# A two-layer trunk on one core: wider loads for the weights' squares, the input scale summed by TensorE, and the place of some memsets

## The chip, the core and the metric

The kernel runs on one core of one Trainium2 chip. The metric is device time in microseconds (us) of one execution. The kernel before took 1095.55 us (median of three runs, 1092.40 to 1097.43). One more execution was taken with the hardware profiler on: 1094.62 us, of which 1092.8 us are the span from the first to the last instruction that the profile shows. Differences of about 0.5% and more can be told from no change.

The engines are named as in the profile: PE is TensorE (PEld its weight loads), DVE is VectorE, ACT is ScalarE, POOL is GpSimd, and SP is the engine that issues most transfers. Each engine works through its own list of instructions in order.

## The reference

A sequence of 1024 tokens, 1024 wide, goes through two layers, each of which adds its result to the residual stream x, and then through a last RMS norm.

```python
def lru_mixer(h, ...):                       # layer 0
    u = h @ w_in                             # 1024 -> 2 * 1536
    xb, gate = u[..., :1536], u[..., 1536:]
    xc = causal_depthwise_conv(xb, conv_w, conv_b)          # 4 taps
    r = sigmoid(block_diag_linear(xc, wa, ba))              # 12 blocks of 128
    i = sigmoid(block_diag_linear(xc, wx, bx))
    log_a = -8.0 * r * softplus(-a_param)
    a = exp(log_a); bterm = sqrt(-expm1(2 * log_a)) * (i * xc)
    hs = scan over time of  s = a * s + bterm
    return (hs * silu(gate)) @ w_out

def fox_mixer(h, ...):                       # layer 1: 16 heads of 64
    u = h @ w_in                             # q, k, v, gate, and 16 forget logits
    cum = cumsum(log_sigmoid(f_logit + b_f))
    logits = q @ k.T / 8 + cum_q - cum_k, causal
    return (softmax(logits) @ v * silu(gate)) @ w_out

for i in range(2):
    h = rms_norm(x, norm_g[i])
    x = x + (lru_mixer if i == 0 else fox_mixer)(h, ...)
return rms_norm(x, final_g)
```

The arithmetic is float32. The kernel splits operands into a high and a low part and multiplies three of the four products (high by high, low by high, high by low).

## The kernel before

Activations lie transposed, channels on the 128 partitions and tokens along the free axis, in two halves of 512 tokens.

**First stage, layer 0 (0 to about 450 us).** A loop over twelve blocks `n` of 128 channels. For each block PE makes `ups` (the block's part of xb, `product`) and `gps` (its gate part), each 48 matmuls of 512 columns, and the two `gate` products. ACT and DVE make the convolution (`xc`), the sigmoids (`th`, `ti`), the recurrence and, a block later, the output y = state times gate, which is split into `yh` and `yl`. After each second block, `project_out` adds that pair's part of y @ w_out to x: the PE matmuls `ops`, which need `yh` and `yl`.

Weights come by a load on SP's queue into a tile `wf` (line 58 or 381), a cast on ACT to the high part `wh` (line 91), and a subtraction on POOL or DVE to the low part `wl` (line 102). The tiles `wf` have three buffers. While layer 0 runs, the list `spare` gives every fourth load one more buffer, with the tag `wx`, in another pool (lines 106 to 110).

Layer 1 works in float16 and needs bounds for its scales: sums of squares of its weights. They are made beside layer 0: `squares_of_weights` (line 407) loads a piece of 256 columns into `wvf` and squares it in place on ACT with `accum_out`, which also leaves the sum of each row. There are 129 such pieces, 32 of `wv`, 96 of `w1` and one of `wf`. They share a tag of two buffers, `wgf`, with the gate weights of `conv`. From block 2 on, the loop takes 4, 5 and 4 of them per block (lines 443, 457 and 466). The load and the square of a piece are written next to each other, so the square is the next user of what was just loaded.

**Between the layers (about 450 to 540 us).** For each half `h` of the tokens the last `ops` are added to x, ACT squares x (`sq`, with the row sums in eight columns of `xsq[h]`), and `input_scale(h)` makes the half's scale: `xsq` times g squared, a reduction of the eight columns to one on DVE (line 531), a sum over partitions by a matmul with ones (`xnorm`), a root (`unit_x`), a reciprocal and `gx`. `split_input(h)` then makes the float16 parts of the half, `hT[h]`, eight casts on ACT and eight on DVE (tiles `h`, line 542). PE goes on with the first of layer 1's projections (`gps`, `vps`). `values(0)` makes `vps`, the values with the forget logits: four tiles of the first half of the tokens, then four of the second, each 24 matmuls. DVE and ACT take them out of PSUM as `v`, and DVE takes the logits as `fz` (line 678). `fixed_rows` writes constants into the attention's operands: T by POOL, U by DVE (lines 603 to 606).

**Second stage, layer 1 (from about 540 us).** Attention head by head, with projections as fill, then the output.

What sets the order. The program is written as Python generators, and a scheduler puts each instruction on its engine's list by priority and by simulated times of its own. `tc.issue_after(x)` places what is written under it after instruction x; `tc.high_priority(offset=...)` raises priority. A buffer is given to its next user when its last reader is done, and the load for the next user waits on SP's queue for that, with everything behind it.

Of the kernel before, what the change touches and what calls it, by code (L numbers as in the profile page):

```python
# [19 lines left out]
P = 128  # L20
# [20 lines left out]
def trunk(ctx: ExitStack, tc: tile.TileContext, xt, w0, wg, wo0, pc, gn, gf, w1, wv, wf, bf, wo1, out):  # L41
# [11 lines left out]
    pe = [None]  # L53
# [137 lines left out]
    with ExitStack() as l0:  # L191
# [7 lines left out]
        spare.append(tmp)  # L199
# [101 lines left out]
        def conv(n, ups):  # L301
# [10 lines left out]
            wt = tmp.tile([P, 2, P], F32, tag="wgf", name="wgf", bufs=2)  # L312
# [94 lines left out]
        def squares_of_weights():  # L407

            todo = [(wv[g, :, k], vsq[:, g, k : k + 1]) for g in range(4) for k in range(KT)]
            todo += [(w1[b, :, 2 * j : 2 * j + 2], wsq[:, 4 * b + j : 4 * b + j + 1]) for b in range(24) for j in range(4)]  # L410
            todo.append((wf, root[:, 1:]))
            for src, to in todo:
                wt = tmp.tile([P, 256], F32, tag="wgf", name="wvf", bufs=2)
                if len(src.shape) == 3:
                    wt = wt[:, : src.shape[1] * src.shape[2]].rearrange("p (a b) -> p a b", b=src.shape[2])
                nc.sync.dma_start(wt, src)
                nc.scalar.activation(wt, wt, AF.Square, accum_out=to)  # L417
                yield

        wsquares = squares_of_weights()  # L420
        ys, fill, held = [], iter(()), {}
        for n in range(NB):
# [19 lines left out]
            if n > 1:  # L442
                take(wsquares, 4)
# [4 lines left out]
            conv(n, both)  # L448
            if n == 0:
# [4 lines left out]
            take(fill, 4)  # L454
            if n > 1:
                with tc.issue_after(state[n - 1]["last"].ins):
                    take(wsquares, 5)
                wn = list(weights(w0[NB + n - 1]))
                gps = held[n - 1] = two_banks("gps")
                for h in range(2):  # L460
                    product(gps[:, h], h, wn)
            if n:
                drain(silu(state[n - 1], held.pop(n - 1)))

                if n > 1:
                    take(wsquares, 4)
                with tc.issue_after(state[n]["tap"].ins):
                    recur(n - 1)
            take(fill, 4)
        gates(NB - 1)  # L470
# [8 lines left out]
        spare.clear()  # L479
# [27 lines left out]
        def weight_bounds():  # L507

            all_ = ps.tile([P, 161], F32, tag="O", name="wnorm")
            matmul(all_[:, 64:160], onesf, wsq, start=True, stop=True)  # L510
# [5 lines left out]
            for cs, to, n in ((slice(0, 64), bounds[:, :8], KT), (slice(64, 160), bounds[:, 8:], 4)):  # L516
# [11 lines left out]
        def input_scale(h):  # L528

            nc.vector.tensor_tensor(xsq[h], xsq[h], g2, ALU.mult)  # L530
# [3 lines left out]
            nc.scalar.activation(unit_x[h], all_, AF.Sqrt, bias=tiny, scale=1.0 / TOP / TOP)  # L534
            nc.vector.reciprocal(xsq[h][:, :1], unit_x[h])
            nc.vector.tensor_scalar(gx[h], gnt[:, 1], xsq[h][:, :1], None, ALU.mult)
# [11 lines left out]
        for h, cs in enumerate(halves):  # L548
# [41 lines left out]
    with ExitStack() as l1:  # L590
# [209 lines left out]
        fixed_rows()  # L800

# [6 lines left out]
        take(first, 8)  # L808
        drain(forget(0))
# [456 lines left out]
```

## Time and profile before

| | |
|---|---|
| runs | 1092.40, 1095.55, 1097.43 us; median 1095.55 |
| profiled execution | 1094.62 us; span 1092.8 us |
| busy in the span | PE 95%, PEld 66%, DVE 72%, ACT 61%, POOL 9% |
| squares of the weights on ACT (line 417) | 129, together 53.3 us, 413 ns each |
| ACT idle just before them, waiting for their loads | 85.6 us |
| first stage: PE busy, 100 to 200 us | 89.21 us |
| first stage: PE busy, 200 to 450 us | 245.95 us |
| between the layers: PE busy, 500 to 510 us | 5.38 us, at a granted clock of 0.66 |

How to read it. PE is busy nearly all the time, so the time can fall where PE waits, where its granted clock is below 1, or where it has less to do. A wait is put down to the instruction that ended last before it. In rows of a timeline the columns are start, duration, engine, line, operation, output and inputs, and count; a bracket gives the idle time before the row and its releaser. A float32 matmul leaves two records in the trace, so eight `sscol` instructions show as x16.

### The profile page before, as it was taken

The numbers are of one execution on the slowest core, as the hardware profiler recorded it, in microseconds if no ns is written. First come the engines' busy times: TensorE is split into PE (matmuls) and PEld (weight loads), VectorE is DVE, ScalarE is ACT, GpSimd is POOL, SyncE is SP. The second block draws the span as 40 slices with busy tenths as digits, with TensorE's granted clock in tenths as the row PEclk, the third lists the DMA queues.
The fourth block names the chain that finished last, engine by engine and source line by source line (L and its number), as shares of the span: only waits on it lengthen the run. The fifth ranks groups of instructions, "written<-read, shape, count | busy, mean of one in ns | idle before, by whom it ended". The sixth has DMA issues, their size and how long they took to land. (4 is left out here: it accounts for less than half of the span.)

```text
span 1092.8 us, 15397 instructions
## 1 busy us (share of the span) xinstructions
PE 1035.4 (95%) x5102; PEld 723.1 (66%) x5102; DVE 791.6 (72%) x1465; ACT 667.9 (61%) x1295; POOL 100.3 (9%) x87
## 2 busy tenths in 40 slices
PE   8998999999999999997899999999999899999997
PEld 6786777788777788765445557544665447577676
DVE  7788465666766768896778884888768884886675
ACT  8579556656565666465666664666556664754454
POOL 1311110222121211001000000000000000011100
PEclk9998999999999999998999999999999999999999
DMA  7212333233223331352578894689948886679994
GB/s 247 78 43 73 107 101 113 75 102 106 86 79 96 89 97 39 116 161 69 148 158 171 171 197 114 140 176 178 194 109 173 181 178 139 132 171 229 253 202 158
DMA packets 229023, 148.94 MB, mean 136 GB/s; under 512 B 162960, under 2 KB 192272, under 8 KB 228944
## 3 DMA queue, kind: packets, MB, share of 16 engines
q1 hardware_dynamic: 226544, 140.10, 52.8%
q0 software_dynamic: 2400, 7.87, 2.4%
q8 instruction: 40, 0.66, 0.3%
q14 instruction: 39, 0.32, 0.1%
HBM read 73.33 MB, written 11.67 MB: 78 GB/s over the span
## 5 line engine op out<-in xcount | busy, mean ns | idle before, releaser
L61 PE MATMUL gps<-h,w 128*128 128x512 f16 x1152 | 270.8, 382 | 2.2 <-DVE qkl L708 2.2
L61 PEld LDWEIGHTS <-w 128*128 128x128 f16 x1152 | 104.5, 98 | 128.6 <-issue 16.8
L861 ACT ACTIVATE p<-S,m 128x128 f32<-128x128 f32 (+7 forms) x128 | 94.2, 736 | 62.7 <-DVE m L856 38.9
L61 PE MATMUL S<-T,U 96*128 96x512 f32 (+7 forms) x384 | 106.2, 386 | 18.3 <-ACT p L861 18.1
L93 ACT ACTIVATE pp<-p,sums 128x128 f16<-128x128 f32 (+7 forms) x128 | 95.5, 770 | 32.8 <-DVE sums L868 11.1
L870 DVE SCALAR_TENSOR_TENSOR pp<-p,sums,pp 128x128 f16<-128x128 f32 (+7 forms) x128 | 102.7, 813 | 14.4 <-ACT pp L93 14.0
L102 POOL TENSOR_TENSOR wl<-wf,wh 128x512 fp32r<-128x512 f32 x46 | 78.9, 1723 | 337.3 <-ACT wh L91 335.8
L417 ACT ACTIVATE wvf<-wvf 128x256 f32<-128x256 f32 x129 | 53.3, 413 | 88.5 <-DMA wvf<-in_w 62.0
L856 DVE CUSTOM_DVE_ANT_0 S<-S,mask 128x128 f32<-128x128 f32 (+7 forms) x128 | 97.1, 759 | 12.3 <-PE S L61 11.1
L61 PEld LDWEIGHTS S<-T,U 128*128 128x128 f32 (+1 forms) x384 | 67.1, 190 | 44.5 <-ACT p L861 30.3
L61 PE MATMUL vps<-w,h 128*128 128x256 f16 (+1 forms) x768 | 88.7, 278 | 6.2 <-DVE fz L678 4.9
L61 PEld LDWEIGHTS <-h 128*128 128x128 f16 x768 | 76.0, 99 | 18.4 <-issue 7.2
L61 PE MATMUL ops<-yh,wh 128*128 128x512 f32 x192 | 77.8, 405 | 10.3 <-DVE x L396 5.6
L61 PE MATMUL ups<-hh,wh 128*128 128x512 f32 x192 | 76.6, 400 | 2.5 <-ACT hh L93 1.5
L61 PE MATMUL gps<-hh,wh 128*128 128x512 f32 x192 | 76.1, 396 | 2.2 <-ACT wh L91 1.8
L617 ACT ACTIVATE w<-wf,wsq 128x512 f16<-128x512 f32 (+1 forms) x74 | 52.4, 717 | 41.9 <-PE gps L61 15.1
L61 PE MATMUL ups<-hh,wl 128*128 128x512 f32 x192 | 76.5, 399 | 1.4 <-POOL wl L102 1.4
L91 ACT CAST wh<-wf 128x512 fp32r<-128x512 f32 x88 | 51.1, 591 | 43.2 <-PE ops L61 25.4
L61 PE MATMUL ups<-hl,wh 128*128 128x512 f32 x192 | 77.0, 402 | 0.2
L61 PE MATMUL ops<-yh,wl 128*128 128x512 f32 x192 | 76.1, 397 | 0.7 <-DVE wl L102 0.7
L61 PE MATMUL gps<-hl,wh 128*128 128x512 f32 x192 | 75.9, 396 | 0.0
L61 PE MATMUL gps<-hh,wl 128*128 128x512 f32 x192 | 75.9, 395 | 0.0
(211 smaller groups left out, 1947.0 us busy)
## 6 DMA issues: line engine op xcount, KB each, us to landing
wf<-in_w SPq DMA_DIRECT2D x106, 256.0 KB
wvf<-in_w SPq DMA_DIRECT2D x96, 128.0 KB
wf<-in_wo SPq DMA_DIRECT2D x64, 128.0 KB
T<-qkh SPq DMA_DIRECT2D x64, 128.0 KB
U<-qkh SPq DMA_DIRECT2D x64, 128.0 KB
x<-in_xt SPq DMA_DIRECT2D x16, 256.0 KB
wvf<-in_wv SPq DMA_DIRECT2D x32, 128.0 KB
x1d<-x SPq DMA_DIRECT2D x16, 256.0 KB
```

The lines of the kernel that those rows point to most:

```text
L61: pe[0] = nc.tensor.matmul(*args, **kw)
L91: cast_last[0] = nc.scalar.copy(hi, src)
L93: nc.scalar.activation(hi, src, AF.Copy, scale=scale)
L102: return eng.tensor_tensor(lo, src, f32(hi), ALU.subtract)
L417: nc.scalar.activation(wt, wt, AF.Square, accum_out=to)
L617: cast_last[0] = nc.scalar.activation(hi, wt, AF.Copy, scale=scales[:, b : b + 1])
L856: nc.vector.tensor_tensor_reduce(S[:, :n], S[:, :n], mask[:, SEQ - n :], -1.0, -NEG, ALU.add, ALU.min, accum_out=m)
L861: seen[0] = nc.scalar.activation(p, S[:, :n], AF.Exp, bias=m, scale=-1.0, accum_out=sums[:, i : i + 1])
L870: nc.vector.scalar_tensor_tensor(both[:, :, 1], p, r, both[:, :, 0], ALU.mult, ALU.subtract)
```

## The change

Four things are changed.

1. Squares of the weights. A piece is now 512 columns wide: 16 loads of `wv` (each squared in two parts of 256), 48 of `w1` (squared in one go) and one of `wf`, so 65 loads and 81 squares. A piece is squared (`measure`) only when the second load behind it has been asked for. The steps are spread over the block: `some()` takes one at seven places (none for blocks 0 and 1), each placed after the ACT instruction that was last written, which wrappers on `nc.scalar.activation` and `nc.scalar.copy` note in `act`. With 48 sums of `w1` for 96, `weight_bounds` reduces pairs.
2. Buffers. The tag `wgf` now holds tiles of 512 columns, still two. The list `spare` is no longer filled, so the loads of weights use the three buffers `wf` alone.
3. Scale. In `input_scale` the reduction on DVE goes; eight matmuls of one column each, summed in PSUM, take its place, for both halves. `input_scale` runs at high priority for both halves, and the second half's splits are written at once, at high priority.
4. `fixed_rows` is written after eight steps of `values(0)` in place of before them.

```diff
+        def noted(op): ...    # act[0] = what the call returns, for nc.scalar.activation and .copy
...
-        spare.append(tmp)
...
-            wt = tmp.tile([P, 2, P], F32, tag="wgf", name="wgf", bufs=2)
+            wt = tmp.tile([P, HALF], F32, tag="wgf", name="wgf", bufs=2)[:, :256].rearrange("p (a b) -> p a b", b=P)
...
-            for src, to in todo:
-                wt = tmp.tile([P, 256], F32, tag="wgf", name="wvf", bufs=2)
-                nc.sync.dma_start(wt, src)
-                nc.scalar.activation(wt, wt, AF.Square, accum_out=to)
+            held = []
+            for src, to in todo + [(None, None)]:
+                if len(held) == 2 or src is None and held:
+                    measure(*held.pop(0))
+                if src is None:
+                    break
+                n = src.shape[1] * src.shape[2]
+                wt = tmp.tile([P, HALF], F32, tag="wgf", name="wsf", bufs=2)[:, :n]
+                nc.sync.dma_start(wt.rearrange("p (a b) -> p a b", b=src.shape[2]), src)
+                held.append((wt, n // len(to), to))
                 yield
+            for h in held:
+                measure(*h)
+                yield
+
+        def measure(wt, n, to):
+            for i, o in enumerate(to):
+                z = wt[:, i * n : i * n + n]
+                last = act[0]
+                nc.scalar.activation(z, z, AF.Square, accum_out=o)
+                act[0] = last
+
+        def some():
+            if n > 1:
+                with tc.issue_after(act[0].ins):
+                    next(wsquares, None)
...
             nc.vector.tensor_tensor(xsq[h], xsq[h], g2, ALU.mult)
-            nc.vector.tensor_reduce(unit_x[h], xsq[h], mybir.AxisListType.X, ALU.add)
             all_ = ps.tile([P, 1], F32, tag="O", name="xnorm")
-            matmul(all_, onesf, unit_x[h], start=True, stop=True)
+            for k in range(KT):
+                matmul(all_, onesf, xsq[h][:, k : k + 1], start=k == 0, stop=k == KT - 1)
...
-            input_scale(h)
+            with tc.high_priority(offset=400):
+                input_scale(h)
             splitting = split_input(h)
+            with tc.high_priority(offset=400):
+                if h:
+                    drain(splitting)
...
-        fixed_rows()
-
         mask = tu.tile([P, SEQ], BF16, name="mask")
...
         take(first, 8)
+        fixed_rows()
         drain(forget(0))
```

From the attention's start to the end of the program the lists of all engines are the same before and after, row by row. They differ in the first stage and between the layers. Three places follow.

First, ACT before the first `ops` of the program: `th` and `ti` are the block's sigmoids, `m` and `a` parts of its recurrence, `yh` the cast that those `ops` need. `wvf` and `wsf` are squares of weights. Before:

```order
L417 ACTIVATE wvf,vsq<-wvf 128x256
L354 ACTIVATE m_1000<-th,c_105 128x1024
L355 ACTIVATE a<-th,nc_106 128x1024
L417 ACTIVATE wvf,vsq<-wvf 128x256 x2
L356 ACTIVATE th<-a 128x1024
L329 ACTIVATE ti<-gate,hbx 128x512
L417 ACTIVATE wvf,vsq<-wvf 128x256
L91 CAST xch<-xc 128x1024
L329 ACTIVATE ti<-gate,hbx 128x512
L91 CAST yh<-a 128x1024
```

and after, from the squares that follow the cast of the block before:

```order
L57 ACTIVATE wsf,vsq<-wsf 128x256 x4
L57 ACTIVATE xc<-us,pct 128x1024
L57 ACT_TABLE_LOAD
L57 ACTIVATE th<-gate,hba 128x512 x2
L57 ACTIVATE wsf,vsq<-wsf 128x256 x2
L57 ACTIVATE m_966<-th,c_105 128x1024
L57 ACTIVATE a<-th,nc_106 128x1024
L57 ACTIVATE wsf,vsq<-wsf 128x256 x2
L57 ACTIVATE th<-a 128x1024
L57 ACTIVATE ti<-gate,hbx 128x512 x2
L57 CAST yh<-a 128x1024
```

Between the earlier `yh` and this one there were nine squares and are now eight; two more now stand ahead of the earlier one; and the cast `xch` now stands behind this `yh`. (All ACT rows of the kernel after carry line 57, the wrapper.)

Second, DVE between the layers, around the second half's scale: `xsq` and `gx` as above, `w` the low parts of layer 1's weights, `qkh` and `qkl` the first projections' parts, `v` the values. Before, up to the reduction:

```order
L530 TENSOR_TENSOR xsq_3646<-xsq_3646,g_3642 128x8
L178 TENSOR_TENSOR sq<-sq 128x512
L618 SCALAR_TENSOR_TENSOR w_4423<-wf,wsq,w_4423 128x512
L102 TENSOR_TENSOR qkl<-gps_4013,qkh 128x512
L99 TENSOR_SCALAR qkh<-gps_4053 128x512
L531 TENSOR_REDUCE unit_x_3648<-xsq_3646 128x1
```

and after, up to `gx`:

```order
L560 TENSOR_TENSOR xsq_3470<-xsq_3470,g_3466 128x8
L186 TENSOR_TENSOR sq<-sq 128x512
L110 TENSOR_TENSOR qkl<-gps_3849,qkh 128x512
L652 SCALAR_TENSOR_TENSOR w_4308<-wf,wsq,w_4308 128x512
L665 SCALAR_TENSOR_TENSOR gps_3889<-gps_3889,wsq,rs_3462 128x512
L652 SCALAR_TENSOR_TENSOR w_4313<-wf,wsq,w_4313 128x512
L107 TENSOR_SCALAR qkh<-gps_3889 128x512
L742 SCALAR_TENSOR_TENSOR qkl<-gps_3889,qkh 128x512
L565 RECIPROCAL xsq_3470<-unit_x_3472 128x1
L566 TENSOR_SCALAR gx_3468<-gnt,xsq_3470 128x8
```

The matmuls `xnorm` need only the first of these rows now. On PE they move forward: before, 70 matmuls `vps` of the first half stand ahead of the second half's `xnorm` and 26 behind it; after, 19 and 77. The values' rows `v`, three of which DVE did ahead of `gx` before, now all stand behind the last split.

Third, DVE behind the last split of the second half, where PE waits for `fz`. Before:

```order
L542 SCALAR_TENSOR_TENSOR h_3826<-x_127,gx_3644,h_3826 128x512
L675 SCALAR_TENSOR_TENSOR v_4149<-vps,rv,v_4149 128x128
L675 SCALAR_TENSOR_TENSOR v_4213<-vps,rv,v_4213 128x128
L605 MEMSET U 64x512
L605 MEMSET U_3987 64x512
L605 MEMSET U_3988 64x512
L678 TENSOR_SCALAR fz<-vps,rf 128x16 x2
```

and after:

```order
L572 SCALAR_TENSOR_TENSOR h_3656<-x_127,gx_3468,h_3656 128x512
L709 SCALAR_TENSOR_TENSOR v_3977<-vps,rv,v_3977 128x128
L709 SCALAR_TENSOR_TENSOR v_4009<-vps,rv,v_4009 128x128
L639 MEMSET U 64x512
L639 MEMSET U_3823 64x512
L639 MEMSET U_3824 64x512
L709 SCALAR_TENSOR_TENSOR v_3980<-vps,rv,v_3980 128x128
L712 TENSOR_SCALAR fz<-vps,rf 128x16
```

The three memsets still stand ahead of the first `fz`, between the same neighbours.

More of the change, by code (lines that the diff above doesn't have):

```diff
@@ L448, in trunk @@
             conv(n, both)
+            some()
             if n == 0:
@@ L454, in trunk @@
             take(fill, 4)
+            some()
             if n > 1:
-                with tc.issue_after(state[n - 1]["last"].ins):
-                    take(wsquares, 5)
                 wn = list(weights(w0[NB + n - 1]))
@@ L509, in weight_bounds @@
             all_ = ps.tile([P, 161], F32, tag="O", name="wnorm")
-            matmul(all_[:, 64:160], onesf, wsq, start=True, stop=True)
+            matmul(all_[:, 64:112], onesf, wsq[:, :48], start=True, stop=True)
             matmul(all_[:, 160:], onesf, root[:, 1:], start=True, stop=True)
```

31 lines of the change are left out of this document (19 added, 12 removed).

## The prediction

> **What bounds the kernel now.** I read the page first, then the waits of PE, then windows and timelines where PE waits.
>
> ```profile
> PE 1035.4 (95%) x5102; PEld 723.1 (66%) x5102; DVE 791.6 (72%) x1465; ACT 667.9 (61%) x1295; POOL 100.3 (9%) x87
> ```
>
> PE has work for 95% of the span. So work that leaves ACT or DVE is worth nothing by itself; a change pays where PE waits, where PE's clock is low, or where PE has less to do. The lists of the engines differ only up to about 530 us, so I ask for PE's waits there. In the first stage they crowd into 100 to 200 us:
>
> ```profile
> PE ops L61 <- ACT yh L91: 4.7, 1, 4.7
> PE ops L61 <- DVE x L396: 2.1, 2, 1.6
> PE gps L61 <- ACT wh L91: 1.8, 1, 1.8
> PE ups L61 <- ACT wh L91: 1.0, 1, 1.0
> PE ups L61 <- POOL wl L102: 0.9, 1, 0.9
> PE gate L61 <- ACT th L329: 0.5, 1, 0.5
> ```
>
> Together 11.0 us (total, times, longest), and all but the 2.1 us are waits for ACT, the 0.9 us by way of POOL. Two of them cost more than their length, as the windows right behind them show (columns: us, then busy time of PE, PEld, DVE, ACT and POOL, granted clock, DMA share, GB/s); the third row is needed further down:
>
> ```profile
> 104.00:109.00 5.00, 4.51 (x10) 3.32 (x11) 4.98 (x5) 4.97 (x11) 1.57 (x2) 0.50 0.08 26
> 129.00:134.00 5.00, 4.91 (x14) 3.52 (x14) 0.00 (x0) 4.62 (x10) 1.08 (x1) 0.66 0.45 131
> 460.00:470.00 10.00, 10.00 (x54) 8.49 (x53) 8.70 (x19) 7.82 (x21) 0.00 (x0) 1.00 0.64 211
> ```
>
> Behind the wait of 4.7 us the granted clock is 0.50 for 5 us, a loss of 2.5 us of work; behind that of 1.8 us it is 0.66, a loss of 1.7. So this stretch loses 11.0 + 2.5 + 1.7 = 15.2 us.
>
> Why is ACT late there, though it is busy only 61% of the span? Its waits, from 100 to 450 us:
>
> ```profile
> ACT wvf L417 <- DMA wvf<-in_w: 62.0, 53, 3.3
> ...
> ACT wvf L417 <- DMA wvf<-in_wv: 16.4, 9, 3.4
> ```
>
> It stands 78.4 us before squares whose loads have not landed, with casts that PE needs queued behind them.
>
> Between the layers PE's timeline shows the other loss:
>
> ```profile
> 483.91 5.72 PE L61 MATMUL vps<-w,h 128*128 128x272 f16 x48
> ...
> 498.57 1.10 PE L61 MATMUL rsrow<-rs,onesf 128*128 128x512 f32 x2 [0.93 <-ACT h L93]
> 504.62 5.53 PE L61 MATMUL vps<-w,h 128*128 128x272 f16 x27 [4.95 <-DVE fz L678]
> ```
>
> PE stands 4.95 us before the second half's values, and the 27 matmuls behind that take 5.53 us where 48 took 5.72: at 0.119 us each they are 3.2 us of work, so 2.3 us go to a low clock.
>
> **Part 1, squares and buffers.** The dearest wait is the 4.7 us for `yh`. ACT ahead of it, and its waits from 84 to 104 us:
>
> ```profile
> 84.76 0.43 ACT L417 ACTIVATE wvf<-wvf 128x256 f32<-128x256 f32 x1
> ...
> 101.47 0.42 ACT L417 ACTIVATE wvf<-wvf 128x256 f32<-128x256 f32 x1 [1.13 <-DMA wvf<-in_wv]
> ...
> 101.89 1.03 ACT L91 CAST xch<-xc 128x1024 fp32r<-128x1024 f32 x1
> 102.82 0.68 ACT L329 ACTIVATE ti<-gate,hbx 128x512 f32<-128x512 f32 x1
> 103.41 1.03 ACT L91 CAST yh<-a 128x1024 fp32r<-128x1024 f32 x1
> ```
>
> ```profile
> ACT wvf L417 <- DMA wvf<-in_wv: 2.2, 3, 1.1
> ```
>
> The first row follows the earlier `yh`. From there to 103.41 ACT does nine squares (84.76 is the first, 101.47 the last) of 0.42 us from start to start (101.47 to 101.89), 3.8 us, and waits 2.2 us for loads: 6.0 us. After, by the order of instructions, ten squares count, eight between and two ahead of the earlier `yh`: 4.2 us, their loads asked for two steps before, so I put their waits at nothing; that gives 1.8 us. The cast `xch`, 0.93 us from start to start, moves behind `yh`. So `yh` comes 2.7 us earlier and about 1.95 us of that wait are left. What the low clock behind it then costs I bound by the rows: 2.5 us, as now, and nothing; I take the middle, 1.25.
>
> The waits for `th`, for DVE's x (DVE itself is held by ACT) and the 1.8 us for `wh` with its 1.7 us of low clock come from squares that wait on their loads, so I let them go. I let the 1.0 and 0.9 us for casts stand: squares still come in bursts of up to six (three loads for two buffers), and the third load of a burst can be asked for only when the first piece is squared. Left are 1.95 + 1.25 + 1.9 = 5.1 us, so the stage gains 15.2 - 5.1 = 10.1 us. Bounds: all of the 15.2, and nothing, if other waits take the places. ACT's work itself, fewer and wider squares, counts nothing: PE's work covers it.
>
> The granted clock is where a rule and a row part. By the Trainium skill, "TensorE: Matmul & The Clock Gate", section "What's actually happening", half clock follows only after at least one idle window of about 3.4 us. By that rule a wait of 1.95 us costs no clock, and the sum would be 1.25 us lower; the trace disagrees, since the 1.8 us wait was followed by 0.66.
>
> The buffer `wx` goes, so a load waits for the low part of the third load before it. A pair of rows, POOL's low parts and a later cast of the same stretch:
>
> ```profile
> 303.52 4.55 POOL L102 TENSOR_TENSOR wl<-wf,wh 128x512 fp32r<-128x512 f32 x2 [15.57 <-ACT wh L91]
> 314.57 0.62 ACT L91 CAST wh<-wf 128x512 fp32r<-128x512 f32 x1 [5.33 <-PE ops L61]
> ```
>
> The second cast, the third behind the first of those low parts, waits for PE to give back a buffer `wh`, not for its load. Its `wf` would come free by 308.1 at the latest, 6.5 us before the cast, and a wait of 3.4 us is the longest that a load of squares caused above. So I put the lost buffer at nothing; what covers it is this slack, and without it each late load costs PE its flight.
>
> **Part 2, the scale by TensorE.** Eight one-column matmuls in place of one, that is sixteen records for two. The nearest row is `sscol`, also one column each, beside the first half's `xnorm`:
>
> ```profile
> 464.38 0.28 PE L61 MATMUL xnorm<-unit_x,onesf 128*128 128x1 f32 x2
> 464.52 1.93 PE L61 MATMUL sscol<-onesf,sq 128*128 128x1 f32 x16
> 466.30 0.48 PE L61 MATMUL ops<-yh,wh 128*128 128x512 f32 x1
> ```
>
> Sixteen take 466.30 - 464.52 = 1.78 us, two take 0.14, so each half gives PE 1.6 us more. In the first half nothing hides that: PE is busy for 10.00 of 10 us from 460 to 470. What DVE saves, one reduction of eight columns, is about the size of the `xsq` row below, 0.16 us, and beside PE's work.
>
> **Part 3, the second half's scale and splits, and U.** The chain that ends PE's 4.95 us, on DVE, and the two ACT rows in it:
>
> ```profile
> 488.82 0.16 DVE L530 TENSOR_TENSOR xsq<-xsq,g 128x8 f32<-128x8 f32 x1
> ...
> 501.87 0.60 DVE L675 SCALAR_TENSOR_TENSOR v<-vps,rv,v 128x128 f16<-128x128 f32 x2
> 502.64 1.57 DVE L605 MEMSET U<- 64x512 f32 x3 [0.16 <-DVE v L675]
> 504.24 0.38 DVE L678 TENSOR_SCALAR fz<-vps,rf 128x16 f32<-128x16 f32 x2
> ```
>
> ```profile
> 490.77 0.72 ACT L617 ACTIVATE w<-wf,wsq 128x512 f16<-128x512 f32 x1 [0.41 <-DMA wf<-in_w]
> ...
> 493.76 0.26 ACT L534 ACTIVATE unit_x<-xnorm,tiny 128x1 f32<-128x1 f32 x1 [0.92 <-PE xnorm L61]
> ```
>
> After, PE reaches `xnorm` behind 19 matmuls: 483.91 + 1.6 + 19 x 0.119 = 487.8. `xsq` is ready near 488.4 (DVE's place in its list moves little, and ACT squares the last x behind one weight cast more). `xnorm` ends at 490.2. ACT's `unit_x` stands behind two more weight casts, the last of which waited for its load until 490.77 before; I take its start at 491.0, between 490.2 and 491.5, so 2.8 us earlier than 493.76. From there to the last split the eight casts of ACT and eight of DVE take as long as before. Then the list shows that the memsets have not moved: 1.57 us still stand ahead of the first `fz`, with one more `v` (0.3) ahead of it. The first `fz` ends at 504.43 (half of the 0.38 for two) - 2.8 + 0.3 = 501.9. PE's own list (`xnorm`, `sscol` and 77 `vps` with `rsrow`, 1.8 + 0.9 + 9.2 + 1.1 us from 488.4) ends at 501.4. So PE goes on at 501.9 for 504.62, 2.7 us earlier with the first half's 1.6 us already in it, and it now waits 0.6 us before `xnorm` and 0.5 here where it waited 0.93 and 4.95. With no wait near 1.8 us the clock stays up, another 2.3 us. Together 5.0 us. Bounds: 4.95 + 0.93 + 2.3 - 1.6 = 6.6 us, if both waits and the low clock go whole, and a loss of 1.6, if only the first half's matmuls come through.
>
> What stands behind: the transposes `fps` of the logits come seven matmuls later (34 behind that point for 27), 0.8 us, and PE's list behind them is the old one, so I put them at nothing; if they delayed the attention, the 0.8 would come back.
>
> **Sum**, against the profiled execution's 1094.62 us: -10.1 - 5.0 = -15.1, so 1079.5 us. The median of the runs lies 0.9 above that execution, so 1080.4; I say 1080.
>
> **Rivals.** A difference of 0.5%, 5.5 us, is about what the measurement can tell from no change, so faster means below 1090.1 and slower above 1101.0.
>
> Loads become the bound (slower). With three buffers a load waits for low parts; on SP's queue it also stands behind loads of squares that wait for ACT, and now these are as large as a weight load. If in each of the ten blocks 2 to 11 one weight load lands late by 3.4 us, the longest wait for a load of squares above, PE loses 34 us, less the 15.1 gained: 1094.6 + 18.9 + 0.9 = 1114. It decides from 1.5 us per block, and is slower by 0.5% from 2.1 us. Against it stands the cast row above, with 6.5 us of room. Chance 0.10.
>
> The first stage keeps its waits (within 0.5%): PE's next partner, DVE, takes ACT's place, as the 2.1 us row hints, or the bursts of squares do. Then only 5.0 us come: 1089.6 + 0.9 = 1090.5. Chance 0.17, half of it below 1090.1.
>
> The new sum does not pay between the layers: `unit_x` waits for the weight casts as before, the memsets stay, and PE has 1.6 us more work. Then -10.1 + 1.6 gives 1087. For it speaks that these casts wait for loads; against it that ACT now has no `v` between them. Chance 0.20.
>
> The forecast holds else, 0.53. Its own range is 1075 to 1086: the 5.1 us that I left in the first stage go too, or, on the other side, the wait for `yh` stays at 4.65 us with its 2.5 us of low clock (2.7 + 1.25) and `unit_x` starts half of its 2.8 us later.
>
> **Range and chances.** Low end: all of the 15.2 and 6.6 us, 1072.8 + 0.9, less half of the 3.2 us by which the lowest run lies under the median, 1072. High end: the first-stage rival with as much on top, 1092. The range 1072 to 1092 leaves out about 2 in 10, most of it above. Faster: 0.53 + 0.20 + 0.08 (half of the first-stage rival) = 0.81, less 0.03 for cases of these three with a small load delay of their own; slower 0.09, most of the load rival; same the rest, 0.13.
>
> **What would show it.** ACT's wait for loads of squares falls from 78.4 us to below 40; PE's wait for `yh` falls to about 2 us, and 129 to 134 us, or the place that answers to it, runs at clock 1. No cast `wh` waits long for a load `wf`; if many do, the buffer was worth its place. `xnorm` shows sixteen records per half at about 0.11 us; the second half's first `vps` behind `fz` starts with a wait below 1 us, and the 27 behind it take about 3.2 us. From the first attention matmul to the end the distance stays what it was. A new run of waits of PE for DVE in 100 to 200 us would make the prediction wrong.

## The result and the profile after

The changed kernel takes 1078.32 us (median of 4 runs, 1075.98 to 1082.82) where the kernel before, run beside it, takes 1096.49: a ratio of 0.9845, with a 95% interval of 0.9802 to 0.9888. The profiled execution took 1077.86 us, with a span of 1076.1. The first part of its page:

```profile
span 1076.1 us, 15162 instructions
PE 1036.2 (96%) x5130; PEld 728.0 (68%) x5130; DVE 789.2 (73%) x1463; ACT 657.7 (61%) x1199; POOL 108.8 (10%) x87
```

PE's waits of the changed kernel from 100 to 540 us (total, times, longest). The waits for ACT's casts, `th` and `yh` are gone from the list; what is left of the first stage is 0.8 us behind a low part of POOL and 0.7 for x (the 0.7 for `wl` come behind it, as before), and of PE's 4.95 us before the second half's values there is 0.5:

```profile
PE gps L69 <- DVE qkl L742: 2.3, 1, 2.3
PE S L69 <- ACT p L57: 1.7, 2, 1.2
PE ups L69 <- POOL wl L110: 0.8, 1, 0.8
PE ops L69 <- DVE wl L110: 0.7, 1, 0.7
PE ops L69 <- DVE x L403: 0.7, 1, 0.7
PE vps L69 <- ACT v L57: 0.5, 1, 0.5
```

ACT's waits for loads of squares (tile `wsf` now, line L57 for all of ACT's instructions), from 20 to 450 us, are 24.3 + 12.1 = 36.4 us where they were 62.0 + 23.6 = 85.6 in the same stretch:

```profile
ACT wsf L57 <- DMA wsf<-in_w: 24.3, 22, 1.8
ACT wsf L57 <- DMA wsf<-in_wv: 12.1, 7, 4.8
```

Three instructions of PE cut both traces into the same pieces: the first `wnorm` (the sum over the weights' squares, so the end of the first stage), the first `xnorm`, and the first `O` (the first product with values in the attention, behind which the lists of all engines are the same in both). Start times in us and distances:

| kernel | wnorm | xnorm | O | span | wnorm to O | O to the end |
|---|---|---|---|---|---|---|
| before | 436.4 | 464.4 | 556.4 | 1092.8 | 120.0 | 536.5 |
| after | 422.9 | 450.9 | 540.2 | 1076.1 | 117.3 | 535.9 |

So the span's 16.7 us come to 13.5 from the first stage, 2.7 from the stretch between the layers, and 0.6 from behind it, which is no more than that part varies by (see below).

Two new losses stand in the trace. One lies in the first stage before 100 us. From 20 us on, the kernel before had waited 0.5 us there until its wait for `yh` began at 99.8 us. PE's timeline shows a wait of 4.46 us for a low part, POOL's timeline shows why, and the windows show the clock behind it (busy times of PE, PEld, DVE, ACT and POOL, then the granted clock, DMA share, GB/s):

```profile
94.26 0.79 PE L69 MATMUL gps<-hh,wl 128*128 128x512 f32 x1 [4.46 <-POOL wl L110]
```

```profile
72.59 1.29 POOL L110 TENSOR_TENSOR wl<-wf,wh 128x512 fp32r<-128x512 f32 x1 [13.55 <-ACT wh L57]
88.52 5.68 POOL L110 TENSOR_TENSOR wl<-wf,wh 128x512 fp32r<-128x512 f32 x1 [14.64 <-ACT wh L57]
```

```profile
95.00:100.00 5.00, 5.00 (x14) 3.89 (x13) 3.90 (x4) 4.19 (x8) 0.00 (x0) 0.52 0.65 210
```

The same subtraction on POOL took 1.29 us at 72.59 and 5.68 us at 88.52; PE waits for it, and then runs at half clock until 99.82 us (from 94.26 to 99.82 the granted clock is 0.50), 2.8 us of work lost. What DVE did at the first of these subtractions, and at the second:

```profile
72.78 2.18 DVE L369 TENSOR_TENSOR ti<-ti,m 128x1024 f32<-128x1024 f32 x1
...
88.00 1.21 DVE L110 TENSOR_TENSOR yl<-a,yh 128x1024 fp32r<-128x1024 f32 x1
89.13 1.22 DVE L369 TENSOR_TENSOR ti<-ti,m 128x1024 f32<-128x1024 f32 x1
90.26 0.68 DVE L110 TENSOR_TENSOR wl<-wf,wh 128x512 fp32r<-128x512 f32 x1
90.87 2.28 DVE L370 TENSOR_TENSOR_SCAN a<-a,ti 128x1024 f32<-128x1024 f32 x1
93.07 2.22 DVE L315 SCALAR_TENSOR_TENSOR xc<-us,pct,xc 128x1023 f32<-128x1023 f32 x1
```

From 88.00 us DVE runs four operations on two tensors back to back, the last of them the scan, which ends at 93.15; POOL's subtraction ends at 94.20, about one ordinary length of 1.29 us later, and in just that time DVE's next operation takes 2.22 us, where the one like it at 74.89 takes 1.27. At the first subtraction POOL began 0.19 us ahead of DVE's operation, and it was DVE that took longer: 2.18 us, where the same operation takes 1.22 at 89.13. It reads as one engine standing still while the other works. The Trainium skill, "GPSIMD Engine Reference", section "8. Key points", says that GpSimd shares its SBUF interfaces with VectorE and that they contend when a DVE instruction has two SBUF inputs; the rows agree. It gives no size; here it is 4.4 us on one operation.

The other new loss is at the eight one-column matmuls. PE's timeline in the first half and the second, and the windows behind each:

```profile
450.87 1.84 PE L69 MATMUL xnorm<-xsq,onesf 128*128 128x1 f32 x16
452.57 1.93 PE L69 MATMUL sscol<-onesf,sq 128*128 128x1 f32 x16
...
475.76 1.92 PE L69 MATMUL xnorm<-xsq,onesf 128*128 128x1 f32 x16
477.54 1.03 PE L69 MATMUL sscol<-onesf,sq 128*128 128x1 f32 x8
```

```profile
454.00:459.00 5.00, 5.00 (x18) 3.79 (x18) 4.55 (x8) 5.00 (x10) 0.00 (x0) 0.66 0.41 116
478.00:483.00 5.00, 5.00 (x32) 3.70 (x32) 4.57 (x16) 2.93 (x7) 0.00 (x0) 0.66 0.32 105
```

PE is busy for all of the time, before, in and behind these records, and yet its clock is 0.66 over the five microseconds that follow: 1.7 us of work lost in each half. In the kernel before, 18 such records stood there and the clock was 1.00 from 460 to 470.

### The profile page after: what moved, and what is told of

It is laid out like the page before. It is cut to its first block, busy times and chain, and to the rows that moved or that the text cites. A ratio compares the mean times of both kernels' runs of the same rounds, so it can differ in the third digit from the quotient of the medians.

```text
span 1076.1 us, 15162 instructions
## 1 busy us (share of the span) xinstructions
PE 1036.2 (96%) x5130; PEld 728.0 (68%) x5130; DVE 789.2 (73%) x1463; ACT 657.7 (61%) x1199; POOL 108.8 (10%) x87
## 5 line engine op out<-in xcount | busy, mean ns | idle before, releaser
L57 ACT ACTIVATE p<-S,m 128x128 f32<-128x128 f32 (+7 forms) x128 | 94.2, 736 | 61.8 <-DVE m L889 37.5
L110 POOL TENSOR_TENSOR wl<-wf,wh 128x512 fp32r<-128x512 f32 x46 | 87.5, 1910 | 315.8 <-ACT wh L57 203.1
L57 ACT ACTIVATE pp<-p,sums 128x128 f16<-128x128 f32 (+7 forms) x128 | 95.5, 770 | 33.2 <-DVE sums L901 12.4
L889 DVE CUSTOM_DVE_ANT_0 S<-S,mask 128x128 f32<-128x128 f32 (+7 forms) x128 | 97.1, 759 | 11.1 <-PE S L69 10.1
L57 ACT CAST wh<-wf 128x512 fp32r<-128x512 f32 x88 | 51.5, 592 | 56.6 <-PE ops L69 31.2
L69 PE MATMUL ops<-yl,wh 128*128 128x512 f32 x192 | 75.6, 400 | 0.0
L57 ACT ACTIVATE w<-wf,wsq 128x512 f16<-128x512 f32 (+1 forms) x74 | 52.4, 717 | 37.8 <-PE gps L69 14.2
```

Of the source, the lines that this page charges most:

```text
L57: act[0] = op(*args, **kw)
L69: pe[0] = nc.tensor.matmul(*args, **kw)
L110: return eng.tensor_tensor(lo, src, f32(hi), ALU.subtract)
L889: nc.vector.tensor_tensor_reduce(S[:, :n], S[:, :n], mask[:, SEQ - n :], -1.0, -NEG, ALU.add, ALU.min, accum_out=m)
```

## The experiments

All times below are medians of 4 to 10 runs, each with the ratio to the kernel before on the same chip and its 95% interval.

**Part 1 alone, and the rest alone.** `squares_alone` is the changed kernel with

```diff
-            for k in range(KT):
-                matmul(all_, onesf, xsq[h][:, k : k + 1], start=k == 0, stop=k == KT - 1)
+            nc.vector.tensor_reduce(unit_x[h], xsq[h], mybir.AxisListType.X, ALU.add)
+            matmul(all_, onesf, unit_x[h], start=True, stop=True)
...
-            with tc.high_priority(offset=400):
-                input_scale(h)
+            input_scale(h)
             splitting = split_input(h)
-            with tc.high_priority(offset=400):
-                if h:
-                    drain(splitting)
```

and `fixed_rows()` back at its old place; `scale_alone` is the kernel before with the reverse of these edits.

> The kernel before with part 1 alone (squares from wide loads two behind, three weight buffers); scale, priority and place of U's memsets as before. My reading: part 1 brings the whole gain of the first stage, so the first wnorm matmul starts at 423 us (before 436.4, after 422.9), PE's wait of 4.5 us behind POOL's low part near 90 us is there, and from wnorm to the first S it takes 97.8 us as before; the time is 13.5 us below the kernel before, about 1082, ratio 0.988. Rival, parts of the gain come from the scale: ratio above 0.993.

Measured: 1082.67 us, ratio 0.9861 (0.9826 to 0.9896). `wnorm` starts at 422.7 us, the wait of 4.5 us near 90 us is there; from `wnorm` to the first `S` (the attention's first matmul) it takes 97.8 us and to `O` 119.9, as before. The first stage's gain is part 1's, all of it.

> The kernel before with parts 2 and 3 alone (eight one-column matmuls for the scale, its splits at high priority, U's memsets written behind the values). My reading: wnorm starts at 436.4 us as before; the 32 one-column records in a row at the first xnorm are followed by some 3 us of granted clock 0.50 although PE never waits, and so are the 24 at the second; wnorm to the first S takes 95.0 us for 97.8, so 1 to 5 us are gained, ratio 0.996 to 0.999. Rival, the two parts only help together: ratio 1.000 or above. Rival, my prediction's sum: 5.0 us, no low clock behind xnorm.

Measured: 1093.07 us, ratio 0.9971 (0.9946 to 0.9995). `wnorm` at 435.7, from there to the first `S` 96.3 us, to `O` 119.9 us, so by the later mark nothing is gained before the attention: between the two marks this run has a stretch of half clock, from 538.8 to 542.2 us, that takes 1.7 us back. The clock falls behind the scale here too, with PE busy throughout:

```profile
466.00:467.00 1.00, 1.00 (x11) 1.00 (x11) 0.75 (x3) 0.52 (x1) 0.00 (x0) 1.00 1.14 258
467.00:468.00 1.00, 1.00 (x5) 0.91 (x5) 0.77 (x2) 1.00 (x4) 0.00 (x0) 0.57 0.56 136
468.00:469.00 1.00, 1.00 (x4) 0.72 (x4) 1.00 (x2) 1.00 (x3) 0.00 (x0) 0.50 0.78 225
469.00:470.00 1.00, 1.00 (x4) 0.81 (x3) 1.00 (x3) 1.00 (x3) 0.00 (x0) 0.50 0.05 9
470.00:471.00 1.00, 1.00 (x5) 0.82 (x4) 1.00 (x2) 1.00 (x3) 0.00 (x0) 0.73 0.29 106
```

The 32 records started at 463.63 us in this run; half clock sets in 3.5 us later and lasts 3.4. The prediction's sum of 5.0 us without a low clock is refuted here.

**The fourth buffer.** The kernel before without `spare.append(tmp)`:

> The kernel before without the fourth weight buffer (wx), nothing else. As predicted, the lost buffer costs nothing: within 1.5 us of the kernel before, and no cast of a weight waits over 1 us for its load. Rival, loads become the bound: from 1.5 us per block in ten blocks, so 1105 or more, with PE waiting for casts wh.

Measured: 1096.22 us, ratio 1.0006 (0.9979 to 1.0032), `wnorm` at 436.7. The buffer costs nothing, as predicted; one cast of a weight waited 1.1 us for its load, which I had put at 1 us at most.

**What of part 1 does it: lag, width or place.** `one_load_behind` changes the one condition

```diff
-                if len(held) == 2 or src is None and held:
+                if len(held) == 1 or src is None and held:
```

> The changed kernel with squares one load behind instead of two. My reading: the lag is what hides the flight of the loads, so ACT's wait for loads of squares rises from 36 us toward 70 (20 to 450 us) and half of the gain of the first stage is lost: 1083 to 1088. Rival, wider loads and their places between the steps do it alone: ACT's wait stays below 45 us and the time is 1076 to 1081.

Measured: 1077.25 us, ratio 0.9823 (0.9786 to 0.9859). ACT's wait does rise, to 43.7 + 9.0 = 52.7 us, and 4.4 more for the one load of `wf`, between what the two expected, but `wnorm` is at 423.7: PE loses 0.8 us, and this run has a stretch of half clock from 8.0 to 11.4 us, 1.7 us of work, that the changed kernel has not. My reading is refuted; the second load in flight is worth nothing to PE. (In flight are two at most: by the diff a square is written just ahead of the second load behind it, not behind that load.) `old_places` keeps wide loads and the lag, and takes the squares where the kernel before did:

```diff
-            some()
+            if n > 1:
+                take(wsquares, 2)
             product(ups[1], 1, wu)
...
             take(fill, 4)
-            some()
             if n > 1:
+                with tc.issue_after(state[n - 1]["last"].ins):
+                    take(wsquares, 3)
...
                 drain(silu(state[n - 1], held.pop(n - 1)))
 
+                if n > 1:
+                    take(wsquares, 2)
                 with tc.issue_after(state[n]["tap"].ins):
                     recur(n - 1)
-                some()
             take(fill, 4)
-            some()
```

(the other two calls of `some()` go as well).

> The changed kernel, its wide loads two behind kept, but the squares taken in bursts of two, three and two at the three places of the kernel before. Theory P, spreading them over the block is what freed ACT: PE's waits for yh, x, wh come back, wnorm starts at 428 us or later, time 1083 or above. Rival W, wider loads and the lag do it: wnorm within 2 us of 422.9 (but for the wait near 90 us), time 1075 to 1081.

Measured: 1072.22 us, ratio 0.9786 (0.9763 to 0.9808), `wnorm` at 421.3. The new places are not what freed ACT. That they cost something doesn't follow: this run hasn't got the wait of 4.5 us near 90 us. Where the low part there is made by DVE in both (below), the stage ends at 417.3 us with the new places and at 421.4 with the old ones, so the new places are worth 4.1 us, and what they brought with them was that wait. `narrow_pairs` is the opposite: the new places and two loads behind, but loads of 256 columns, two at each place.

```diff
-                (wv[g, :, k : k + 2], [vsq[:, g, k + i : k + i + 1] for i in range(2)])
-                for g in range(4)
-                for k in range(0, KT, 2)
+                (wv[g, :, k : k + 1], [vsq[:, g, k : k + 1]])
+                for g in range(4)
+                for k in range(KT)
...
-                    next(wsquares, None)
+                    take(wsquares, 2)
```

> The changed kernel with the squares' loads of 256 columns again, two of them at each of the new places, two behind. Theory P (places): ACT's wait for loads of squares stays below 50 us from 20 to 450 us and wnorm starts within 2 us of 422.9, time 1076 to 1081. Rival W (width): ACT's wait is 60 us or more, wnorm at 428 or later, time 1083 or above.

Measured: 1095.62 us, ratio 0.9999 (0.9977 to 1.0022), `wnorm` at 442.3 us, 6 us later than in the kernel before. ACT's and PE's waits, from 20 us on:

```profile
ACT wsf L57 <- DMA wsf<-in_w: 66.5, 37, 4.4
ACT wsf L57 <- DMA wsf<-in_wv: 21.6, 11, 3.2
```

```profile
PE gate L69 <- ACT th L57: 9.0, 6, 2.8
PE gps L69 <- POOL wl L110: 4.0, 3, 3.1
PE ups L69 <- POOL wl L110: 1.9, 3, 1.1
```

ACT stands 88.1 us before loads, as before the change, although they are asked for two behind and at the new places. So the width is the cause: with all else kept, `wnorm` comes 19.4 us later without it, and neither the lag nor the places can stand in for it. There are 65 wide loads or 129 narrow ones, and ACT waits 36.4 us before the ones and 88.1 before the others. That it sits through flights in proportion to their number is my reading of these two sums; wide loads with neither the lag nor the new places were not run.

**The wait near 90 us.** `low_part_on_dve`:

```diff
-                wn = list(weights(w0[NB + n - 1]))
+                wn = list(weights(w0[NB + n - 1], lo_eng=nc.vector if n == 3 else nc.gpsimd))
```

> The changed kernel with the two low parts of the fourth block's gate weights made by DVE instead of POOL. My reading: PE's wait of 4.5 us near 90 us comes from a POOL low part that DVE's operations stretch from 1.3 to 5.7 us; on DVE it takes 0.68 us, so the wait and the 2.4 us of low clock behind it go: wnorm's first matmul at 416 to 418 us (422.9 in the changed kernel), time 1072. Rival, the load or the cast is late, or DVE, which is busy all the time there, becomes the one that PE waits for: wnorm at 421 or later.

Measured: 1069.55 us, ratio 0.9759 (0.9727 to 0.9791), the fastest of all, below both kernels. `wnorm` at 417.3. The wait of 4.5 us is gone, and so is the low clock behind it; PE's waits in the first stage from 20 us on are now

```profile
PE ops L69 <- ACT yh L57: 1.5, 1, 1.5
PE ups L69 <- ACT wh L57: 0.5, 1, 0.5
PE ups L69 <- POOL wl L110: 0.4, 1, 0.4
```

The 5.6 us that `wnorm` gains on the changed kernel are about the 4.5 + 2.8 us less the 1.5 for `yh`, 5.8. `old_places_and_low_part` puts this edit into `old_places`.

> The changed kernel with the squares at the three places of the kernel before and the fourth block's gate weights' low parts on DVE. My reading: the two remove the same wait near 90 us, so they do not add: wnorm at 417 to 421 us, time 1067 to 1072. Rival, the old places gain somewhere else: wnorm at 415 or earlier, time 1064 or below.

Measured: 1079.4 us, ratio 0.9841 (0.9814 to 0.9868), `wnorm` at 421.4: in the first stage they do not add, as expected, but the time lies above the expected 1067 to 1072. From `O` to the end this run takes 541.1 us, `low_part_on_dve` 533.4, with the same lists there. The difference is in the clock. In windows of 5 us from `O` to 10 us before the end, `low_part_on_dve` has none below 1.00; this kernel has three, at these places (same columns as above):

```profile
657.00:662.00 5.00, 3.60 (x11) 1.71 (x12) 3.41 (x9) 3.45 (x8) 0.00 (x0) 0.73 0.36 121
787.00:792.00 5.00, 4.61 (x15) 2.15 (x16) 3.76 (x10) 3.85 (x8) 0.00 (x0) 0.70 0.32 85
1007.00:1012.00 5.00, 5.00 (x17) 3.97 (x16) 4.12 (x15) 2.41 (x8) 0.55 (x1) 0.66 1.07 347
```

Each is a stretch of 3.4 us at half clock, which the first two rows cut short: 1.7 us of work, 5.1 in all. Counted the same way, the fourteen kernels lose 0, 1.7, 3.4 or 5.1 us behind `O`, and the time from `O` to the end goes up with it: 533.4 us with none; 534.1 to 536.5 with one such stretch; 535.9 to 538.7 with two; 539.1 to 542.5 with three. That is over half of the 9.1 us by which the profiled executions differ there, so where the marks and the medians below disagree, I go by the marks.

**The one-column matmuls.** `reduction_back` undoes part 2 alone (the first two lines of the diff above), `wide_column` keeps eight matmuls and moves each column 64 times:

```diff
-                matmul(all_, onesf, xsq[h][:, k : k + 1], start=k == 0, stop=k == KT - 1)
+                matmul(all_, onesf, xsq[h][:, k : k + 1].to_broadcast([P, 64]), start=k == 0, stop=k == KT - 1)
```

> The changed kernel with part 2 alone undone: DVE adds up the eight columns, one one-column matmul per half; priority and memsets as changed. My reading: with 18 one-column records in a row in the first half and 10 in the second, the granted clock stays at 1 behind them, which gives 3.3 us back in the first half; but the second xnorm then stands behind 70 values' matmuls again instead of 19, so PE waits some 4 us for fz: wnorm to the first S 94 to 97 us (95.0 in the changed kernel), time 1077 to 1080. Rival, the priority moves the splits without part 2: wnorm to S 92 or less, time 1075. Rival, the low clock has nothing to do with these matmuls: it is still there behind the first xnorm.

Measured: 1077.5 us, ratio 0.9832 (0.9805 to 0.9858). The clock stays up behind the first `xnorm`, and PE's wait for `fz` is back:

```profile
450.00:455.00 5.00, 5.00 (x33) 4.43 (x32) 5.00 (x12) 4.92 (x12) 0.00 (x0) 1.00 0.63 204
455.00:460.00 5.00, 5.00 (x23) 2.75 (x22) 5.00 (x14) 5.00 (x10) 0.00 (x0) 1.00 0.62 170
...
487.00:492.00 5.00, 4.75 (x27) 3.38 (x28) 4.69 (x16) 0.49 (x3) 3.77 (x4) 0.66 0.82 182
```

```profile
487.25 5.54 PE L69 MATMUL vps<-w,h 128*128 128x272 f16 x32 [3.95 <-DVE fz L712]
```

From `wnorm` to `O` it takes 117.2 us, the changed kernel 117.3. Its time is the one that my reading expected. In these two runs part 2 is worth nothing: what it gives by letting the scheduler put the second `xnorm` behind 19 matmuls instead of 70, its own records and the low clock behind them take back.

> The changed kernel, but each of the eight scale matmuls moves its column 64 times (128x64 for 128x1), so that PE's array streams more between the loads of weights; same number of records. Theory A, the clock falls because one-column matmuls leave the array almost idle: the granted clock stays at 1 behind the first xnorm with its sscol, a record takes no longer than 0.13 us, and 1.7 us come back in each half: wnorm to the first S 91.6 to 93 us (95.0 in the changed kernel), time 1075. Rival B, it falls by the number of such fp32 records in a row or by something outside PE: again 0.50 for some 3 us, time 1078 or above.

Measured: 1078.42 us, ratio 0.9838 (0.9811 to 0.9865). Behind the second `xnorm` (16 wide records, 8 narrow) the clock stays at 1; behind the first (16 wide, 16 narrow) it falls again, as the windows show:

```profile
452.00:453.00 1.00, 1.00 (x9) 1.00 (x9) 0.52 (x4) 0.85 (x3) 0.00 (x0) 0.77 0.74 197
453.00:454.00 1.00, 1.00 (x3) 0.84 (x4) 0.59 (x1) 1.00 (x2) 0.00 (x0) 0.50 0.83 257
454.00:455.00 1.00, 1.00 (x4) 0.78 (x3) 0.31 (x1) 1.00 (x3) 0.00 (x0) 0.50 0.34 81
```

`wnorm` to the first `S` is 94.6 us and to `O` 117.7, so nothing is won. Sixteen narrow records alone never brought the clock down (below), so the wide ones ahead of them counted too: 64 columns are not enough to be taken for work, and theory A falls as I had put it. Over all fourteen kernels: 18 one-column records in a row (five kernels) were never followed by a low clock; 24 in a row were in five of eight; 32 in a row in seven of eight. `old_places_and_low_part` has 32 and 24 and no low clock behind either. So a long run makes the fall likely and not certain.

What decides the single case can be read from the same traces. In each of the fourteen every stretch of half clock starts a whole number of steps of 3.413 us behind the one before it, and lasts one step or two (the one at the end of the program, where PE stops, aside). Where this grid of steps lies is different in each run. In the changed kernel the three steps around the first half's scale are:

```profile
451.39:454.80 3.41, 3.41 (x30) 3.36 (x31) 2.93 (x7) 2.70 (x8) 0.00 (x0) 1.00 0.73 226
454.80:458.21 3.41, 3.41 (x10) 2.65 (x9) 3.41 (x6) 3.41 (x7) 0.00 (x0) 0.50 0.31 87
458.21:461.62 3.41, 3.41 (x16) 1.84 (x16) 3.41 (x7) 3.12 (x7) 0.00 (x0) 1.00 0.21 77
```

Of the 32 one-column records 26 start in the first of them, and the next one runs at half clock. Counted like this in all the kernels but `wide_column`, a step at full clock in which 20 to 32 such records start was followed by half clock all twelve times, and one with 18 or fewer never. In `old_places_and_low_part`, which kept its clock, the grid cut the 32 into 16 and 16 and the 24 into 8 and 16. So the fall goes with how many start in one step, and for a run of 24 or 32 that hangs on where the grid lies, which no kernel here set. In `wide_column` a step with 16 wide and 14 narrow records was followed by half clock and one with 16 wide and 5 narrow was not, though 20 narrow ones were enough elsewhere: a wide record may count for less, which two cases don't show.

`no_priority` takes the priority away and drains the splits late:

```diff
-            with tc.high_priority(offset=400):
-                input_scale(h)
+            input_scale(h)
             splitting = split_input(h)
-            with tc.high_priority(offset=400):
-                if h:
-                    drain(splitting)
```

> The changed kernel without the high priority and with the second half's splits drained behind the row of scales as before; eight matmuls and memsets as changed. The second xnorm still stands behind 24 values' matmuls (19 in the changed kernel). My reading: the priority by itself is worth 0 to 1.5 us: wnorm to the first S 95 to 96.5 us, time 1078 to 1080. Rival, it carries the gain between the layers: wnorm to S 97.5 or more, time 1081.

Measured: 1077.44 us, ratio 0.9819 (0.9786 to 0.9852). `wnorm` to the first `S` is 97.4 us, to `O` 119.1 where the changed kernel has 117.3. That lies between what my reading and the rival expected, and it isn't the priority's worth: PE stands idle as long in both (5.3 us from `wnorm` to `O`), and 1.7 of the 1.8 us are one more stretch of half clock, as the second half's lasts from 478.1 to 484.9 us here and half as long in the changed kernel. Whether the priority or the place of the grid did that is not shown, and the runs' medians can't tell that size.

**A version with both mends.** `fused_sum_and_low_part` has the low part on DVE, and the product and the sum in one DVE operation:

```diff
-            nc.vector.tensor_tensor(xsq[h], xsq[h], g2, ALU.mult)
+            nc.vector.tensor_tensor_reduce(
+                xsq[h], xsq[h], g2, 1.0, 0.0, ALU.mult, ALU.add, accum_out=unit_x[h]
+            )
...
-            for k in range(KT):
-                matmul(all_, onesf, xsq[h][:, k : k + 1], start=k == 0, stop=k == KT - 1)
+            matmul(all_, onesf, unit_x[h], start=True, stop=True)
```

> The changed kernel with the fourth block's gate weights' low parts on DVE and with the product by g2 and the sum of the eight columns in one DVE operation, so that one one-column matmul per half is left; the second xnorm stands behind 47 values' matmuls. My reading: wnorm at 417 to 418, clock 1 behind the first xnorm, wnorm to the first S 92 to 94.5 us: time 1066 to 1069, below both kernels. Rival, the later second xnorm eats what the matmuls give: wnorm to S 95 to 97, time 1070 to 1072.

Measured: 1074.57 us, ratio 0.9801 (0.9775 to 0.9826). `wnorm` at 417.6 and clock 1 behind the first `xnorm`, but `wnorm` to `S` is 94.5 us and to `O` 116.7 (116.3 in `low_part_on_dve`). PE's timeline:

```profile
483.30 5.51 PE L69 MATMUL vps<-w,h 128*128 128x272 f16 x34 [4.42 <-DVE fz L713]
```

The time lies above what either expected. The rival holds for the mechanism: the second `xnorm`, behind 48 matmuls instead of 14, brings back a wait of 4.4 us for `fz`, and the matmuls saved are spent on it.

## Why the prediction came out, step by step

**The first stage: 10.1 us predicted, 13.5 measured; the direction and the place were right, the reason given was not.** ACT's waits for loads fell below the 40 us named, and PE's waits for ACT went with them; 129 to 134 us and the place that answers to it run at clock 1. The step that fails is that the squares' waits vanish because their loads are "asked for two steps before": with one load behind the stage ends 0.8 us later, which one more stretch of half clock at 8 us covers; with narrow loads two behind it ends 19.4 us later. It is the width, which the prediction counted only as work of ACT and put at nothing.

Two terms were mis-sized by it. The waits that I let stand, 1.95 us for `yh` with 1.25 of low clock and the casts' 1.9, are 0.8 in the trace. And the sum stopped at 200 us, while behind it 3.3 us went too (4.1 us of PE's idle time from 200 to 450 us became 0.8). Against both stands the loss that I did not see, 4.5 + 2.8 us at 90 to 100 us. I read POOL's low parts for their end, 308.1, and not for why two of them took 4.55 us when one alone takes 1.3; that row was the warning. By rows, PE's idle time up to `wnorm` fell by 9.5 us (18.3 to 8.8) and what it lost at half clock by 1.6 (4.4 to 2.8); another 2.4 us of the 13.5 I can't place.

**The lost buffer at nothing** holds: 1.0006 without it. **Loads as the bound** did not come.

**Part 2: 1.6 us a half predicted, 3.3 measured.** The records' own price was right: `sscol` starts 452.57 - 450.87 = 1.70 us behind `xnorm`, 0.14 before. What failed is that the prediction put nothing else to their account, and for the second half the sentence that "the clock stays up": 32 and 24 such records in a row, 26 and 24 of them in one step of the grid, cost 1.7 us of clock in each half.

**Part 3 and the sum of 5.0 us: 2.7 measured.** The chain went as worked out. The second `xnorm` stood behind 19 matmuls, the memsets stayed ahead of `fz`, PE waited 0.53 us there as against 0.5 predicted, and the 21 `vps` from 491.83 took 2.60 us, 0.12 each. The 3.4 us missing are the two low clocks; the wait of 1.26 us for `qkl`, which I had not counted, went too: 5.0 - 3.4 + 1.3 = 2.9. The rival that the scale does not pay between the layers is right for part 2 by itself (117.2 without it, 117.3 with it), and for the priority it stays open, since one more stretch of half clock makes up the 1.8 us that `no_priority` is longer.

**The attention unchanged**: 536.5 and 535.9 us.

**The total** of 1080 for 1078.3 is thus in part luck: 3.4 us too little from the first stage and 2.3 too much between the layers nearly cancel.

**The rule on the clock.** The Trainium skill, "TensorE: Matmul & The Clock Gate", section "What's actually happening", says that the gate goes by how busy PE has been in a free-running window of about 3.4 us. The traces agree: all stretches of half clock start on a grid of 3.413 us and last one step of it or two, and each step costs 1.7 us where PE has work. That an idle window of 3.4 us is needed does not agree. I counted the steps at full clock, from 30 us to about 10 us before the end, in all fourteen traces. All 39 in which PE stood idle for over 57.5% were followed by half clock, and so were 6 of the 37 in which it did for 48.5 to 57.5%, and 13 in which 20 or more of the scale's short records started; of the other 4070 none was. The wait of 1.78 us in the kernel before lay whole within one step and was followed by half clock; that of 1.48 us in `low_part_on_dve` lay in one step too, and was not. My middle of 1.25 us for a wait of 1.95 was not tried, since no such wait came; by this count the price of a wait is nothing or 1.7 us for each step, and which of them it is can hang on where the grid lies.

## What to carry to other kernels

When an engine sits before a stream of small loads with a fixed number of buffers, count flights before anything else: halving the number of loads, with all else kept, moved the end of the stage by 19.4 us here, where asking one load earlier was worth nothing and the new places 4.1 us, once the wait that came with them was gone. When one operation on POOL takes longer than its twins, look at what DVE runs on two tensors at that time, and give the one that PE waits for to DVE. Tiny matmuls in a long run cost more than their records: look at the granted clock behind them, not only at PE's busy column. And where two traces differ by 1.7 us or twice that, look for one more stretch of half clock before you give the difference to a change.

## What the hardware showed that was not expected

- PE at 100% busy with one-column fp32 matmuls can be followed by half clock: 32 records (3.5 us) seven times out of eight, 24 records (2.7 us) five out of eight, 18 records (1.9 us) never in five. The loss is 1.7 us, once 3.4 (`no_priority`, second half).
- Stretches of half clock lie on a grid of 3.413 us that has another place in each run. A step of it with 20 or more one-column records was followed by half clock twelve times out of twelve, with 18 or fewer never; one without such records always when PE stood idle for over 57.5% of it, and never when for under 48.5%.
- A subtraction of 128x512 on POOL took 5.68 us instead of 1.29 while DVE ran three operations on two tensors and a scan back to back; DVE's next operation was held in turn (2.22 us for 1.27).
- One column or 64 make next to no difference to how long a record takes here: sixteen records of 128x64 took 1.90 us in `wide_column`, sixteen of 128x1 took 1.84.
- With the same lists on all engines, `O` to the end took 533.4 to 542.5 us over the fourteen kernels, in step with zero to three stretches of half clock of 1.7 us each.
